# Sample states of a hybrid decoder: from one sequence a step to 128-row chunks of four sequences, with outer products in row groups of the array

## The chip, the cores and the metric

One core of a Trainium2 chip runs the whole program. The metric is the time of one execution in microseconds of the device; three runs of the kernel before the change have a median of 2565.08 us. A difference of some 0.2% (5 us) can be told from none.

## The reference, cut to what matters

One layer of a decoder is computed for a prompt of 512 tokens and for eight sample sequences of four tokens each (32 sample tokens), together 544 columns. Both go through one input projection and then through two branches, an mLSTM and a sliding-window attention, which are merged. The part that changes here is the mLSTM of the sample sequences: each of 8 sequences and 4 heads has a state matrix C of 512 x 512 numbers in f32 (1 MB), which is read, used and written back:

```
num   = s @ v + inter * (q @ C)          # q: 4 tokens of the sequence
den   = sum(s) + inter * (q @ n)
h     = num / max(|den|, exp(-m_row))
C_new = decay * C + (w * k).T @ v        # a sum of four outer products
n_new = decay * n + sum(w * k)
```

So for each head and sequence there is a readout q @ C, and an update of C by a product whose contraction runs over the four tokens of that sequence alone.

## The kernel before

Weights are streamed from memory in pieces of 1024 x 128. A piece is split by ScalarE and VectorE into a high and a low part (`wh`, `wl`, type fp32r), and a product of f32 precision is made of three fp32r products (wh with both parts of the input, wl with the high part). The input projection runs in pairs of column blocks by Strassen's scheme with seven products: `paired` goes through 72 pairs, each of seven half products, and a half product is 24 matmuls of 128 x 128 by 272 columns (L597 with wh, L599 with wl). Two buffers each for wh and wl let the splits run up to two half products ahead.

All other work is written as generators. After each half product `tick()` advances every live generator by one `yield`, so a `yield` is worth one half product of TensorE's time. TensorE keeps the order in which the program is written (`manual_schedule`); the orders of VectorE, ScalarE, GpSimd and the DMA queue are made by a scheduler that simulates the program, and each engine then runs its list strictly in order.

The sample stage (`samples`, `sample_head`) runs beside the later pairs (its TensorE work stands from half product 282 to 487 of 504), head after head:

- `sample_prep` loads q, k, v and n of the 32 sample tokens, repeats k four times over the 128 rows (`rep`, by GpSimd, one quarter for each of four parts), makes scores against q (L969), transposes (L974), and builds `kA`, `Pst` and `V4`: rows of weighted k, of scores and of v in which the four groups of 32 rows hold hi or lo parts, so that one contraction over 128 rows sums the products hi*hi, hi*lo, lo*hi and lo*lo of all 32 tokens.
- Then eight steps, one for each sequence b. GpSimd makes `qz` (q with all but the sequence's columns zero, L1064 and L1065) and `Ab` (`kA` masked to the sequence, L1067). Four half products later TensorE makes the readout (L1079): four f32 products, one for each 128 rows of C, in the four column groups of the array, and they add up in one bank `pC` over all eight steps. Behind it come four outer products (L1085), two at once and two one half product later, each of 128 rows by 128 columns by 512; VectorE adds each to the state (L1086).
- `sample_finish` scales the readout (L1028), sums the four groups by a product with a selection matrix (L1035), adds `num`, normalises by rows (`layernorm_rows`, the tiles `lns`, `lnst`; its last step on ScalarE is L930), and transposes (L1043) three half products later.

States are loaded one step ahead (`load_C`, 1 MB, two buffers) and stored as two DMAs of 512 KB. `sm()` gives one of four banks of PSUM in turn. When all heads are done, the stage's memory is given back and eleven tiles `pf` of the next stage's input are fetched ahead.

Of the kernel before, what the change touches and what calls it, by code (L numbers as in the profile page):

```python
# [21 lines left out]
SEQ = 512  # L22
# [17 lines left out]
SLOPES = [float(np.float32(2.0 ** (-8.0 * (h + 1) / AH))) for h in range(AH)]  # L40


C_ID, C_TRI, C_DIST, C_SB, C_M8, C_SM, C_SEL, C_Q, C_N = 0, 128, 256, 512, 644, 652, 684, 716, 844


def constants():
    c = np.zeros((128, C_N), np.float32)
    p = np.arange(128)
    c[:, C_ID:C_ID + 128] = np.eye(128)
    c[:, C_TRI:C_TRI + 128] = np.where(p[None, :] >= p[:, None], 0.0, NEG)  # L50
    dist = p[:, None] + 128 - np.arange(256)[None, :]
    c[:, C_DIST:C_DIST + 256] = np.where((dist >= 0) & (dist < 128), dist, 1.0e32)
    t = p % 4
    sd = 128 + t[:, None] - np.arange(132)[None, :]
    slope = np.array(SLOPES, np.float32)[p // 4]
# [5 lines left out]
    same = (tok[:, None] // 4 == tt[None, :] // 4) & (tok[:, None] <= tt[None, :])  # L61
    c[:, C_SM:C_SM + 32] = np.where(same, 0.0, NEG)
    c[:, C_SEL:C_SEL + 32] = (tok[:, None] == tt[None, :])
    c[:, C_Q:C_Q + 128] = np.where(tok[:, None] == tok[None, :], 0.25, 0.0)
    return c

# [7 lines left out]
def _build(tc, nc, i, o, es):  # L74
# [83 lines left out]
    dcb = cst.tile([128, MH, NB], F32, name="dcb")  # L158
    dcc = cst.tile([8, MH], F32, name="dcc")
    m8r = cst.tile([128, 8], F32R, name="m8r")  # L160

    d_brm = dr.tile([16, 128, T], F32, name="d_brm")
    d_bra = dr.tile([16, 128, T], F32, name="d_bra")
# [149 lines left out]
    V.memset(r32(m8r[:]), 0.0)  # L313
    for q in (0, 2):
        A.copy(m8r[q * 32:q * 32 + 32], cc[q * 32:q * 32 + 32, C_M8:C_M8 + 8])


    def gates_half(ps, half):
# [19 lines left out]
    def gates(ps):  # L338
# [85 lines left out]
        V.tensor_copy(T1[96:100, 0:128], A3)  # L424

        reps = []
        for src in (T2, T1):
            rep = ev(128)
            V.tensor_copy(rep[:].rearrange("p (r t) -> p r t", r=4),
                          src[:, SEQ:T].unsqueeze(1).to_broadcast([128, 4, NS]))  # L430
            reps.append(rep)
        for _ in range(4):
            yield
        for src, rep, dst, m in ((T2, reps[0], colT2, 3), (T1, reps[1], colT1, 4)):
            pt, pt2 = sm(), sm()
            for b in range(4):
                PE.transpose(pt[:, b * 128:b * 128 + 128], src[:, b * 128:b * 128 + 128], ident)
            PE.transpose(pt2[:, 0:128], rep[:], ident)
            V.tensor_copy(dst[:, 0:4], pt[:].rearrange("p (b d x) -> p b d x", b=4, d=4)[:, :, 0:m, 0:4])
            V.tensor_copy(dst[:, 4], pt2[:, 0:128].rearrange("p (d x) -> p d x", d=4)[:, 0:m, 0:4])  # L440
        pd = sm()
# [502 lines left out]
    def w512():  # L944
        return sp["sw"].tile([128, 512], F32, tag="w", name=nm("w"))

    def load_C(h, b):
        ct = sp["sC"].tile([128, 4, 512], F32, tag="C", name=nm("C"))
        nc.sync.dma_start(ct[:], i["state_mlstm_C"][b, h].rearrange("(c p) v -> p c v", p=128))
        return ct  # L950

    def sample_prep(h, r):
        qs = st1([128, 4, NS], "qs", p="sw")
# [6 lines left out]
        nc.sync.dma_start(nh, i["state_mlstm_n"][:, h, :])  # L960
        yield
        yield
        rep = st1([128, 4, 4, NS], "rep")
        G.tensor_copy(rep[:], ks_[:].unsqueeze(2).to_broadcast([128, 4, 4, NS]))
        yield

        pS, pb = sm(), sm()
        for c in range(4):
            PE.matmul(pS[:, 0:NS], rep[:, c].rearrange("p r t -> p (r t)"), qs[:, c], start=(c == 0), stop=(c == 3))  # L969
        PE.matmul(pb[:, 0:NS], cc[0:4, C_ID + h:C_ID + h + 1].to_broadcast([4, 128]), nM[:, SEQ:T],  # L970
                  start=True, stop=True)
        pk = sm()
        for c in range(4):
            PE.transpose(pk[:, c * 128:c * 128 + 128], rep[:, c].rearrange("p r t -> p (r t)"), ident)  # L974
        ds = st1([128, NS], "ds")
        V.tensor_tensor(out=ds[:], in0=pb[:, 0:NS], in1=cc[:, C_SM:C_SM + NS], op=ALU.add)
        A.activation(ds[:], ds[:], AF.Exp, bias=colT1[:, 4, 0, h:h + 1])
        V.tensor_tensor(out=ds[:], in0=pS[:, 0:NS], in1=ds[:], op=ALU.mult)
        Pst = st1([128, NS], "Pst", F32R)
        A.copy(Pst[:], ds[:])  # L980
        V.tensor_tensor(out=Pst[64:128], in0=ds[64:128], in1=r32(Pst[64:128]), op=ALU.subtract)

        wcol = colT2[:, 4, 2, h:h + 1]
        kA = st1([128, 512], "kA", F32R)
        A.activation(kA[:], pk[:], AF.Copy, scale=wcol)
        V.scalar_tensor_tensor(kA[64:128], pk[64:128], wcol[64:128], r32(kA[64:128]), op0=ALU.mult, op1=ALU.subtract)
        repv = st1([128, 4, 4, NS], "rep")
        G.tensor_copy(repv[:], vs[:].unsqueeze(2).to_broadcast([128, 4, 4, NS]))
        yield

        pvv = sm()
        for c in range(4):
            PE.transpose(pvv[:, c * 128:c * 128 + 128], repv[:, c].rearrange("p r t -> p (r t)"), ident)
        V4 = st1([128, 512], "V4", F32R)
        A.copy(V4[:], pvv[:])
        for q in (1, 3):
            rr = slice(q * 32, q * 32 + 32)
            V.tensor_tensor(out=V4[rr], in0=pvv[rr], in1=r32(V4[rr]), op=ALU.subtract)

        pn = sm()  # L1000
        for c in range(4):
# [18 lines left out]
        pN = sm()  # L1020
        PE.matmul(pN[:NS, :], Pst[:], V4[:], start=True, stop=True)
        num = st1([128, 4, 4, NS], "rep")[:32].rearrange("p c r t -> p (c r t)")
        A.copy(num, pN[:NS, :])
        r.update(kA=kA, V4=V4, den=den, num=num, qs=qs)

    def sample_finish(h, r, pC):
        qc = w512()
        A.activation(qc[:], pC[:], AF.Copy, scale=colT2[:, 4, 1, h:h + 1])  # L1028
# [4 lines left out]
        num, den = r["num"], r["den"]  # L1033
        pI = sm()
        PE.matmul(pI[:NS, :], cc[:, C_SEL:C_SEL + 32], qc[:], start=True, stop=True)  # L1035
        V.tensor_tensor(out=num, in0=pI[:NS, :], in1=num, op=ALU.add)
        hn = w512()[:32]
        layernorm_rows(NS, den[:, 9:10], colT2[0:32, 4, 0, h:h + 1], [num], hn, sp["sw"])
        for _ in range(3):
            yield  # L1040
        pt = sm()
        for c in range(4):
# [3 lines left out]

    def sample_head(h):
        r = {}
        nxt = load_C(h, 0)
        yield from sample_prep(h, r)  # L1050
        pC, stores = None, []
# [8 lines left out]
        for b in range(NB):  # L1060
            ct = nxt

            qz = st1([128, 4, NS], "qz", p="sw")
            G.memset(qz[:], 0.0)  # L1064
            G.tensor_copy(qz[:, :, b * 4:b * 4 + 4], r["qs"][:, :, b * 4:b * 4 + 4])  # L1065
            Ab = st1([128, 512], "Ab", F32R)
            G.tensor_scalar(Ab[:], r32(r["kA"][:]), cc[:, C_M8 + b:C_M8 + b + 1], None, op0=ALU.mult)  # L1067
            for j in range(4):
                yield
                if j == 0:  # L1070
                    store()
                elif j == 2 and b + 1 < NB:
                    with tc.issue_after(state["load"].ins):
                        nxt = load_C(h, b + 1)
            if b == 0:
                pC = sm()

            for c in range(4):
                PE.matmul(pC[c * 32:c * 32 + 32, :], qz[:, c], ct[:, c],  # L1079
                          start=(b == 0), stop=(b == NB - 1), tile_position=(0, c * 32))  # L1080
            for c in range(4):
                if c == 2:
                    yield
                pu = sm()
                PE.matmul(pu[:], Ab[:, c * 128:c * 128 + 128], r["V4"][:], start=True, stop=True)  # L1085
                V.scalar_tensor_tensor(ct[:, c], ct[:, c], dcb[:, h, b:b + 1], pu[:], op0=ALU.mult, op1=ALU.add)  # L1086
                if c % 2:
                    stores.append((C_s[b, h, (c - 1) * 128:c * 128 + 128, :].rearrange("(c p) v -> p c v", p=128),
                                   ct[:, c - 1:c + 1]))
        yield  # L1090
        store()
        while h not in gated:
            yield
        yield from sample_finish(h, r, pC)

    chain_, gated = [], []
    esF, ahead, PF = ExitStack(), [], 11
# [505 lines left out]
```

## Time and profile before

| What | Value |
|---|---|
| Runs | 2562.29, 2565.08, 2566.04 us |
| Profiled execution | span 2561.7 us; no other time is given for it |
| Paired stage | 88.7 us to 1825.4 us (L597 first start, end of the last L599's eight) |
| Sample stage, first load of C to the last transposes | 1047.2 us to 1774.0 us |
| Readouts L1079 | 256 records (each f32 product counts twice), 592/605/617 ns (min/median/max) |
| Outer products L1085 | 128 records, 387/396/498 ns |
| State additions L1086 (VectorE) | 128, 742 ns median |

A row of the timeline holds the start, how long the merged group lasted, the engine, the line, and out<-in with the tiles' shapes; `128*32` is the size of the stationary operand (rows*columns). Since matmuls overlap, the spacing of starts says what each costs. PEld is the load of weights. A row ends with the engine's idle time before it and what released it. A row of a table by windows holds the busy time of each engine with its number of instructions, then the granted clock of TensorE, the busy share of the DMA engines and GB/s.

### The profile page before, as it was taken

How to read it: one execution, taken by the hardware profiler on the slowest of the kernel's cores; microseconds unless marked ns; L12 is line 12 of the kernel's file. 1: busy time of each engine (PE TensorE's matmuls, PEld its weight loads, DVE VectorE, ACT ScalarE, POOL GpSimd, SP SyncE). 2: the span in 40 equal slices, each digit the busy share in tenths (PEclk: the TensorE clock that was granted, in tenths of full speed). 3: DMA queues.
4: the chain of work that ended last, by engine and by line, in shares of the span. 5: the costliest groups of instructions: out<-in, count | busy, mean ns of one | idle time of the engine just before them, and what ended most of it. 6: DMA issues, size and time to landing. Idle time of an engine off the chain costs nothing.

```text
span 2561.7 us, 48818 instructions
## 1 busy us (share of the span) xinstructions
PE 2524.2 (99%) x19994; PEld 2464.3 (96%) x19994; DVE 1707.2 (67%) x2508; ACT 1173.2 (46%) x1908; POOL 362.3 (14%) x334
## 2 busy tenths in 40 slices
PE   8999999999999999999999999999999999999997
PEld 8999999999999999899999998999999999999997
DVE  7867777777777777687777877777856553333236
ACT  4447667666666655333433433434633332222221
POOL 2111211211111111121121222221000000000002
PEclk9999999999999999999999999999999999999999
DMA  6566666666666663477576575676655455446332
GB/s 196 139 160 157 151 156 154 152 158 148 157 160 146 156 161 89 119 230 235 154 236 212 168 227 163 185 235 207 187 171 172 162 179 155 139 135 189 106 97 86
DMA packets 537103, 421.86 MB, mean 165 GB/s; under 512 B 43536, under 2 KB 449344, under 8 KB 536592
## 3 DMA queue, kind: packets, MB, share of 16 engines
q1 hardware_dynamic: 526800, 382.04, 49.8%
q0 software_dynamic: 10080, 36.70, 7.9%
q8 instruction: 157, 2.57, 0.4%
q14 instruction: 66, 0.54, 0.1%
HBM read 297.66 MB, written 86.42 MB: 150 GB/s over the span
## 4 chain that ended last, share of the span: by engine, by line
PE 57%; DVE 1%; issue 0%; POOL 0%; ACT 0%; DVEq 0%
PE mm L200 21%; PE bank L597 17%; PE bank L599 9%; PE sm L1266 2%; PE sm L1085 1%; PE sm L1079 1%; PE sm L1298 1%; PE sm L1311 1%; PE sm L200 1%; DVE z L1505 0%; PE sm L1245 0%; PE sm L1321 0%; PE sm L1253 0%; DVE z L1510 0%; PE sm L1448 0%
## 5 line engine op out<-in xcount | busy, mean ns | idle before, releaser
L191 ACT CAST wh<-raw 128x1024 fp32r<-128x1024 f32 x604 | 632.8, 1048 | 978.5 <-PE bank L597 599.3
L192 DVE TENSOR_TENSOR wl<-raw,wh 128x1024 fp32r<-128x1024 f32 x604 | 750.1, 1243 | 367.3 <-ACT wh L191 359.9
L597 PE MATMUL bank<-xk,wh 128*128 128x272 f32 x2304 | 312.7, 288 | 1.3 <-DVE ev L622 1.3
L597 PEld LDWEIGHTS bank<-xk,wh 128*128 128x128 f32 x2304 | 297.7, 188 | 4.2 <-ACT wh L191 2.4
L577 DVE TENSOR_TENSOR raw<-raw,raw 128x1024 f32<-128x1024 f32 x218 | 276.5, 1270 | 5.5 <-DMA raw<-in_w_in 2.9
L200 PE MATMUL mm<-bh,wl 128*128 128x272 f32 x1024 | 214.0, 289 | 0.0
L200 PE MATMUL mm<-bh,wh 128*128 128x272 f32 x1024 | 213.6, 290 | 0.0
L200 PE MATMUL mm<-bl,wh 128*128 128x272 f32 x1024 | 213.3, 288 | 0.0
L599 PE MATMUL bank<-xk,wl 128*128 128x272 f32 x1152 | 168.1, 288 | 0.0
L616 POOL TENSOR_TENSOR ev<-p,ev 128x272 f32<-128x272 f32 x72 | 105.0, 1458 | 424.9 <-ACT ev L615 404.4
L200 PEld LDWEIGHTS mm<-bh,wh 128*128 128x128 f32 x1024 | 160.7, 188 | 2.3 <-issue 2.3
L200 PEld LDWEIGHTS mm<-bl,wh 128*128 128x128 f32 x1024 | 161.4, 188 | 0.0
L200 PEld LDWEIGHTS mm<-bh,wl 128*128 128x128 f32 x1024 | 160.9, 189 | 0.0
L599 PEld LDWEIGHTS bank<-xk,wl 128*128 128x128 f32 x1152 | 153.4, 189 | 0.0
L597 PE MATMUL bank<-n2h,wh 128*128 128x272 f32 x576 | 149.1, 290 | 1.9 <-ACT wh L191 1.9
L597 PE MATMUL bank<-s1h,wh 128*128 128x272 f32 x576 | 150.5, 292 | 0.0
L597 PE MATMUL bank<-s1l,wh 128*128 128x272 f32 x576 | 149.3, 292 | 0.0
L597 PE MATMUL bank<-s4h,wh 128*128 128x272 f32 x576 | 149.0, 290 | 0.0
L597 PE MATMUL bank<-a11h,wh 128*128 128x272 f32 x576 | 148.7, 290 | 0.0
L597 PE MATMUL bank<-n2l,wh 128*128 128x272 f32 x576 | 148.7, 291 | 0.0
L597 PE MATMUL bank<-a11l,wh 128*128 128x272 f32 x576 | 148.5, 291 | 0.0
L597 PE MATMUL bank<-n3l,wh 128*128 128x272 f32 x576 | 148.2, 290 | 0.0
(427 smaller groups left out, 5489.7 us busy)
## 6 DMA issues: line engine op xcount, KB each, us to landing
raw<-in_w_in SPq DMA_DIRECT2D x296, 512.0 KB, 4.4
raw<-raw POOLq DMA_DIRECT2D x70, 512.0 KB, 4.9
C<-in_state_mlstm_C SPq DMA_DIRECT2D x32, 1024.0 KB, 5.6
out<-C SPq DMA_DIRECT2D x64, 512.0 KB, 3.8
raw<-in_w_proj_a SPq DMA_DIRECT2D x32, 512.0 KB, 5.6
raw<-in_w_proj_m SPq DMA_DIRECT2D x32, 512.0 KB, 4.3
raw<-in_w_out SPq DMA_DIRECT2D x32, 512.0 KB, 4.3
d_sgm<-ev SPq DMA_DIRECT2D x16, 272.0 KB, 3.9
```

Source lines behind the costliest of these rows:

```text
L191: A.copy(wh[:], raw[:])
L192: V.tensor_tensor(out=wl[:], in0=raw[:], in1=r32(wh[:]), op=ALU.subtract)
L200: PE.matmul(ps[:, f, :w], a[:, kk], b(k, c, w), start=(k == 0 and n == 0), stop=(k == 15 and n == 2))
L577: V.tensor_tensor(out=w[out][:], in0=w[a][:], in1=w[b][:], op=ALU.add)
L597: PE.matmul(ps, wh[:, k], x(p, k), start=(first and k == 0 and p == 0), stop=False, skip_group_check=True)
L599: PE.matmul(ps, wl[:, k], x(0, k), start=False, stop=(k == 7), skip_group_check=True)
L616: G.tensor_tensor(out=c22, in0=p1, in1=c11, op=ALU.subtract)
L1079: PE.matmul(pC[c * 32:c * 32 + 32, :], qz[:, c], ct[:, c], start=(b == 0), stop=(b == NB - 1), tile_position=(0, c * 32))
L1085: PE.matmul(pu[:], Ab[:, c * 128:c * 128 + 128], r["V4"][:], start=True, stop=True)
L1266: PE.matmul(pp[:, 0:258], a[:, b * 128:b * 128 + 128], b_[:, b, f], start=(b == 0 and n == 0), stop=(b == 3 and n == 2))
L1298: PE.matmul(pp[:, 0:n], x_[c][:, b * 128:b * 128 + 128], y_[c][:, b * 128:SEQ], start=(c == 0 and m == 0), stop=(c == 3 and m == 2))
L1311: PE.matmul(pp[:, 0:258], x_[:, off:off + 128], y_[:, b, f], start=(b == 0 and n == 0), stop=(b == j and n == 2))
```

## The change

A step no longer takes one sequence with all 512 rows of its C, but 128 rows (chunk c) of four sequences: the even ones for s = 0, then the odd ones for s = 1. `load_C` fetches four blocks of 128 x 512, again 1 MB, and the stores are again two of 512 KB.

```
-    def load_C(h, b):
+    def load_C(h, s, c):
         ct = sp["sC"].tile([128, 4, 512], F32, tag="C", name=nm("C"))
-        nc.sync.dma_start(ct[:], i["state_mlstm_C"][b, h].rearrange("(c p) v -> p c v", p=128))
+        nc.sync.dma_start(ct[:], i["state_mlstm_C"][s::2, h, c * 128:c * 128 + 128, :].rearrange("b p v -> p b v"))
```

The rows of `kA`, `V4` and `Pst` are ordered anew: row group b holds 16 rows (four tokens by four parts) of sequence 2b and 16 of 2b + 1, and `Ab` masks one of the two by s, so it is made twice a head and not eight times. Building the rows takes two ScalarE passes and one VectorE pass:

```
+    def rows_of_parts(out, hi, ps, at, scales):
+        low = st1([128, 512], "rep")
+        A.activation(hi[:], ps[:], AF.Copy, scale=scales[0])
+        A.activation(low[:], ps[:], AF.Copy, scale=scales[1])
+        V.scalar_tensor_tensor(out[:], r32(hi[:]), cc[:, at:at + 1], low[:], op0=ALU.mult, op1=ALU.add)
```

The step itself: the readout of a chunk goes to a bank of its own, is copied out by ScalarE and added up by GpSimd in `sum`; one half product later the four outer products follow together, each with a contraction over the 32 rows of one row group and into a bank of its own.

```
-            for c in range(4):
-                PE.matmul(pC[c * 32:c * 32 + 32, :], qz[:, c], ct[:, c],
-                          start=(b == 0), stop=(b == NB - 1), tile_position=(0, c * 32))
-            for c in range(4):
-                if c == 2:
-                    yield
-                pu = sm()
-                PE.matmul(pu[:], Ab[:, c * 128:c * 128 + 128], r["V4"][:], start=True, stop=True)
-                V.scalar_tensor_tensor(ct[:, c], ct[:, c], dcb[:, h, b:b + 1], pu[:], op0=ALU.mult, op1=ALU.add)
+                pC = sm()
+                for b in range(4):
+                    PE.matmul(pC[b * 32:b * 32 + 32, :], qz[:, b], ct[:, b], start=True, stop=True,
+                              tile_position=(0, b * 32))
+                if (s, c) == (0, 0):
+                    r["sum"] = st1([128, 512], "rep")
+                    A.copy(r["sum"][:], pC[:])
+                else:
+                    some = w512()
+                    A.copy(some[:], pC[:])
+                    G.tensor_tensor(out=r["sum"][:], in0=r["sum"][:], in1=some[:], op=ALU.add)
+                yield
+                pus = [sm() for _ in range(4)]
+                for b in range(4):
+                    rows = slice(b * 32, b * 32 + 32)
+                    PE.matmul(pus[b][:], Ab[rows, c * 128:c * 128 + 128], r["V4"][rows], start=True, stop=True,
+                              tile_position=(b * 32, 0))
+                for b in range(4):
+                    V.scalar_tensor_tensor(ct[:, b], ct[:, b], dcb[:, h, b * 2 + s:b * 2 + s + 1], pus[b][:],
+                                           op0=ALU.mult, op1=ALU.add)
```

`qz` takes four small copies and not one. In `sample_prep` one `yield` is added behind each of the two copies of `rep`, and the one ahead of the product Pst * V4 falls away: that product moves into `sample_finish`, where it adds to the selection product in the same bank, so `num` is gone. In `sample_finish` five half products and not three lie between the normalisation and the transposes. A head thus takes 55 half products and not 52, counted from head to head. In the constants the mask of scores and some columns are laid out anew, and the gates make one more transposed copy of a column (`colW`).

**The order on TensorE at one step.** Before, in the third step of the first head: the end of a half product, the readout (L1079), two outer products (L1085), the next half product.

```order
L599 MATMUL bank_13251<-n3h_122,wl_13247 128x272 x8
L1079 MATMUL sm_12968<-C_13118,qz_13205 32x512 x4
L1085 MATMUL sm_13349<-V_1690_12734,Ab_13208 128x512
L1085 MATMUL sm_13352<-V_1690_12734,Ab_13208 128x512
L597 MATMUL bank_13215<-s4h_1010,wh_13277 128x272
L597 MATMUL bank_13215<-s4l_1011,wh_13277 128x272
```

With the change, in the third step of the first head (L610 and L612 are the old L597 and L599, L1101 is the readout), the readout stands alone:

```order
L612 MATMUL bank_13216<-s4h_1009,wl_13297 128x272 x8
L1101 MATMUL sm_13393<-C_13169,qz_13257 32x512 x4
L610 MATMUL bank_13268<-xk_5_112,wh_13329 128x272
L610 MATMUL bank_13268<-xk_7_114,wh_13329 128x272
L610 MATMUL bank_13268<-xk_5_112,wh_13329 128x272
```

One half product later all four outer products (L1114) stand together:

```order
L612 MATMUL bank_13268<-xk_5_112,wl_13330 128x272 x4
L612 MATMUL bank_13268<-xk_6_113,wl_13330 128x272 x4
L1114 MATMUL sm_13438<-V_1703_12810,Ab_12866 128x512
L1114 MATMUL sm_13439<-V_1703_12810,Ab_12866 128x512
L1114 MATMUL sm_13440<-V_1703_12810,Ab_12866 128x512
L1114 MATMUL sm_13441<-V_1703_12810,Ab_12866 128x512
L610 MATMUL bank_13461<-a11h_108,wh_13364 128x272
L610 MATMUL bank_13461<-a11l_109,wh_13364 128x272
```

Two visits a step remain, but the second pair has moved from one to the other.

**The order at the end of the third head.** Before, on VectorE, the last two steps of the normalisation (L925, L926) stand behind the split wl_18472:

```order
L922 SCALAR_TENSOR_TENSOR lns_18391<-lns_18391 32x1
L192 TENSOR_TENSOR wl_18436<-raw_2477_18433,wh_18435 128x1024
L923 TENSOR_SCALAR lns_18391<-lns_18391 32x1
L192 TENSOR_TENSOR wl_18472<-raw_18325,wh_18471 128x1024
L925 TENSOR_TENSOR lns_18391<-lns_18391 32x1
L926 SCALAR_TENSOR_TENSOR lns_18391<-lns_18391 32x1
```

and on TensorE the transposes (L1043) stand behind the half product that reads wl_18405, from whose buffer wl_18472 has to be made, two splits later:

```order
L597 MATMUL bank_18475<-a11l_108,wh_18404 128x272
L599 MATMUL bank_18475<-a11h_107,wl_18405 128x272 x8
L1043 MATMUL sm_18502<-cc,w_18390 128x32 x4
L597 MATMUL bank_18524<-s1h_118,wh_18435 128x272
L597 MATMUL bank_18524<-s1l_119,wh_18435 128x272
```

With the change the same steps (L938, L939) stand behind the split wl_18843:

```order
L199 TENSOR_TENSOR wl_18807<-raw_2543_18804,wh_18806 128x1024
L938 TENSOR_TENSOR lns_18762<-lns_18762 32x1
L199 TENSOR_TENSOR wl_18843<-raw_18696,wh_18842 128x1024
L939 SCALAR_TENSOR_TENSOR lns_18762<-lns_18762 32x1
L199 TENSOR_TENSOR wl_18874<-raw_2536_18731,wh_18873 128x1024
```

and the transposes (L1064) stand behind the half product that reads wl_18843 itself:

```order
L610 MATMUL bank_18912<-n2l_122,wh_18842 128x272
L612 MATMUL bank_18912<-n2h_121,wl_18843 128x272 x8
L1064 MATMUL sm_18938<-cc,w_18761 128x32 x4
L610 MATMUL bank_18846<-xk_5_112,wh_18873 128x272
L610 MATMUL bank_18846<-xk_7_114,wh_18873 128x272
```

The chain's end has moved ahead of the transposes by two half products, as counted in splits of wl.

**The order on VectorE at one step.** Before, the four additions to the state (L1086) stand in two pairs with other work between:

```order
L192 TENSOR_TENSOR wl_13313<-raw_1742_13062,wh_13312 128x1024
L1086 SCALAR_TENSOR_TENSOR C_13118<-C_13118,dcb,sm_13349 128x512
L1086 SCALAR_TENSOR_TENSOR C_13118<-C_13118,dcb,sm_13352 128x512
L577 TENSOR_TENSOR raw_1785_13395<-raw_13281,raw_13283 128x1024
L577 TENSOR_TENSOR raw_13283<-raw_13283,raw_1775_13316 128x1024
L624 SCALAR_TENSOR_TENSOR ev_13241<-bank_13215,ev_13241 128x272
L192 TENSOR_TENSOR wl_13356<-raw_13281,wh_13355 128x1024
L1086 SCALAR_TENSOR_TENSOR C_13118<-C_13118,dcb,sm_13384 128x512
L1086 SCALAR_TENSOR_TENSOR C_13118<-C_13118,dcb,sm_13387 128x512
```

With the change (L1117) they stand in one piece, behind the split for the half product two ahead:

```order
L199 TENSOR_TENSOR wl_13404<-raw_1787_13401,wh_13403 128x1024
L1117 SCALAR_TENSOR_TENSOR C_13169<-C_13169,dcb,sm_13438 128x512
L1117 SCALAR_TENSOR_TENSOR C_13169<-C_13169,dcb,sm_13439 128x512
L1117 SCALAR_TENSOR_TENSOR C_13169<-C_13169,dcb,sm_13440 128x512
L1117 SCALAR_TENSOR_TENSOR C_13169<-C_13169,dcb,sm_13441 128x512
L199 TENSOR_TENSOR wl_13458<-raw_13300,wh_13457 128x1024
```

All four have moved behind one split, and nothing stands between them.

More of the change, by code (lines that the diff above doesn't have):

```diff
@@ L1018, in sample_prep, with sample_finish @@
         nc.sync.dma_start(n_s[:, h, :], nh)
-        yield
[L1020 to L1026, printed above, removed]
+        r.update(kA=kA, V4=V4, Pst=Pst, den=den, qs=qs)
+    def sample_finish(h, r):
         qc = w512()
-        A.activation(qc[:], pC[:], AF.Copy, scale=colT2[:, 4, 1, h:h + 1])
+        A.activation(qc[:], r["sum"][:], AF.Copy, scale=colT2[:, 4, 1, h:h + 1])
         gs = st1([128, 4, NS], "gs", p="sw")
@@ L1032, in sample_finish @@
         yield
[L1033 removed]
         pI = sm()
[L1035 to L1036 removed]
+        PE.matmul(pI[:NS, :], cc[:, C_SEL:C_SEL + 32], qc[:], start=True, stop=False)
+        PE.matmul(pI[:NS, :], r["Pst"][:], r["V4"][:], start=False, stop=True)
         hn = w512()[:32]
[L1038 to L1039 removed]
+        layernorm_rows(NS, r["den"][:, 9:10], colT2[0:32, 4, 0, h:h + 1], [pI[:NS, :]], hn, sp["sw"])
+        for _ in range(5):
             yield
```

118 lines of the change are left out of this document (67 added, 51 removed).

## Prediction

> **What bounds the kernel now.** I read the page's busy shares first, then its chain of work that ended last, then a table of busy time for a stretch inside the sample stage, and then the timeline of TensorE, instruction by instruction.
>
> ```profile
> span 2561.7 us, 48818 instructions
> PE 2524.2 (99%) x19994; PEld 2464.3 (96%) x19994; DVE 1707.2 (67%) x2508; ACT 1173.2 (46%) x1908; POOL 362.3 (14%) x334
> PE 57%; DVE 1%; issue 0%; POOL 0%; ACT 0%; DVEq 0%
> ...
> core 0: us, PE busy (x) PEld busy (x) DVE busy (x) ACT busy (x) POOL busy (x), PEclk, DMA share, GB/s
> 1200.00:1400.00 200.00, 198.82 (x1533) 185.74 (x1531) 153.10 (x183) 75.31 (x93) 36.43 (x38) 1.00 0.66 207
> ```
>
> TensorE is busy from end to end, and in the sample stage nearly all the time, while VectorE has 47 us of 200 free, ScalarE 125 and GpSimd 164. So a microsecond of TensorE's own sequence is a microsecond of the kernel, as long as nobody makes TensorE wait. Busy time hides two things, though: pipelined products overlap, so their spacing counts and not their length; and TensorE works at half clock after a long wait. Both need the timeline.
>
> ```profile
> 1080.65 1.16 PE L599 MATMUL bank<-a11h,wl 128*128 128x272 f32 x8
> 1081.65 0.29 PE L597 MATMUL bank<-s1h,wh 128*128 128x272 f32 x1
> ...
> 1083.66 1.16 PE L599 MATMUL bank<-s1h,wl 128*128 128x272 f32 x8
> 1084.75 1.06 PE L1079 MATMUL sm<-C,qz 128*32 128x512 f32 x8
> 1085.74 0.72 PE L1085 MATMUL sm<-V,Ab 128*128 128x512 f32 x2
> 1086.31 0.29 PE L597 MATMUL bank<-n2h,wh 128*128 128x272 f32 x1
> ...
> 1088.32 1.16 PE L599 MATMUL bank<-n2h,wl 128*128 128x272 f32 x8
> 1089.32 0.63 PE L1085 MATMUL sm<-V,Ab 128*128 128x512 f32 x2
> 1089.79 2.17 PE L597 MATMUL bank<-xk,wh 128*128 128x272 f32 x16
> 1091.80 0.42 PE L599 MATMUL bank<-xk,wl 128*128 128x272 f32 x2
> ```
>
> The first column is the start. Eight pair products take 1.00 us (1080.65 to 1081.65), sixteen 2.01 (1089.79 to 1091.80), so 0.125 us each and 3.0 us for a half product of 24. One step of a sample head is what stands between them: 0.09 us to enter (1.09 instead of 1.00 before 1084.75), 0.99 for the readouts, 0.57 for two outer products, and in the next visit 0.47 for the other two: 2.12 us, and 32 steps make 68 us.
>
> **The outer products.** Today four products of 512 columns run one after the other; 0.47 us for a pair gives 0.235 us each. The first of a step costs 0.10 more, since it follows the readouts. Without that, which the readouts cause, four cost 0.94 us. After the change each has a contraction of 32 rows and its own row group and bank. Do groups run side by side? The trace has that for columns, and once for rows of 64 together with columns of 32:
>
> ```profile
> L1079 PE MATMUL sm<-C,qz x256: 592/605/617, 1084.7 to 1749.9; 128*32 128x512 f32 x128
> ...
> L1085 PE MATMUL sm<-V,Ab x128: 387/396/498, 1085.7 to 1754.2; 128*128 128x512 f32 x128
> ...
> 954.03 0.44 PE L856 MATMUL sm<-kT,qas 64*32 64x128 f32 x8
> ```
>
> Eight readout products of 605 ns stand within 1.06 us (the f32 product counts twice), so four run at a time; at 954.03 eight products of 64 rows lie within 0.44. I take it that four row groups overlap in the same way. Then an outer visit is one product, 0.235 us, plus about 0.03 for three staggered starts, plus X, the price of changing to row groups and back. No row shows X for fp32r products. Two rows bound it:
>
> ```profile
> 1072.40 0.39 PE L1021 MATMUL sm<-V,Pst 128*32 128x512 f32 x1
> 1072.63 0.28 PE L597 MATMUL bank<-s4h,wh 128*128 128x272 f32 x1
> ...
> 1217.99 1.16 PE L599 MATMUL bank<-s4h,wl 128*128 128x272 f32 x8
> 1219.08 1.04 PE L1035 MATMUL sm<-w,cc 128*32 128x512 f32 x2
> 1220.06 2.28 PE L597 MATMUL bank<-xk,wh 128*128 128x272 f32 x16
> 1222.18 1.17 PE L599 MATMUL bank<-xk,wl 128*128 128x272 f32 x8
> ```
>
> L1021, a narrow fp32r product without a position in the array, costs 0.23 us in all: X is zero. L1035, f32, is entered 0.09 late, lasts 0.98 where the readouts' first pass (half of it) implies about 0.89, and the sixteen products behind it take 2.12 instead of 2.01: 0.29 us for a round trip. I take X = 0.25, near the second, because it also changes what the array is set to. An outer visit then costs 0.235 + 0.03 + 0.25 = 0.52 us, 0.42 less than 0.94, and 32 of them save **13.3 us** (with X from 0 to 0.29: 21.6 to 12.3). The readouts keep their eight products and their round trip of 0.29, now paid towards pair products instead of the first outer product: no change.
>
> [...]
>
> **The waits.** The added half products stand between dependent pieces of a head's start and end. Here the trace has three waits:
>
> ```profile
> 1052.38 1.18 PE L599 MATMUL bank<-s1h,wl 128*128 128x272 f32 x8
> 1057.38 1.92 PE L969 MATMUL sm<-qs,rep 128*128 128x32 f32 x8 [3.82 <-POOL rep L964]
> ...
> 1228.21 1.16 PE L599 MATMUL bank<-s1h,wl 128*128 128x272 f32 x8
> 1230.55 0.43 PE L1043 MATMUL sm<-cc,w 32*128 32x32 f32 x4 [1.18 <-ACT w L930]
> ...
> 1587.09 1.16 PE L599 MATMUL bank<-a11h,wl 128*128 128x272 f32 x8
> 1592.13 0.63 PE L1043 MATMUL sm<-cc,w 32*128 32x32 f32 x4 [3.89 <-ACT w L930]
> ...
> 1057.40:1062.80 5.40, 5.40 (x24) 5.27 (x25) 1.24 (x4) 1.11 (x3) 0.90 (x2) 0.50 0.47 115
> ...
> 1592.10:1598.70 6.60, 6.57 (x30) 6.51 (x31) 0.39 (x2) 1.20 (x2) 0.61 (x1) 0.50 0.23 60
> ...
> 1588.41 2.03 DVE L192 TENSOR_TENSOR wl<-raw,wh 128x1024 fp32r<-128x1024 f32 x1 [0.18 <-ACT wh L191]
> 1590.90 0.15 DVE L925 TENSOR_TENSOR lns<-lns 32x1 f32<-32x1 f32 x1 [0.46 <-POOL lns L924]
> ```
>
> Starting from the end of the eight (start plus 1.00), TensorE lost 4.0, 1.3 and 4.0 us. Behind the two long ones the granted clock is 0.50 for 5.4 and 6.6 us. There 24 and 30 products stand, 0.22 us apart instead of 0.125, so 43% of each stretch is lost: 2.3 and 2.8. Together **14.4 us**.
>
> The last two belong to the end of a head: VectorE's normalisation chain (L925, L926) stands behind the split wl of the second next half product, and that split needs a buffer that TensorE frees only when it reaches the transposes L1043. TensorE waits for a chain that had waited for TensorE. In the changed order two more half products lie between. For the third head the chain stands behind wl_18843, which the half product just ahead of the transposes reads itself; its buffer is free two half products, 6 us, earlier, and the 4.0 us go with 2 to spare. The other heads read alike, so 1.3, 4.0 and 2.8 go. At the first head's start one half product (3.0 us) is added ahead of L969, but GpSimd makes four more small copies ahead of rep there:
>
> ```profile
> 1056.71 0.61 POOL L964 COPY rep<-ks 128x512 f32<-128x512 f32 x1
> ...
> L1065 POOL COPY qz<-qs 128x16 f32<-128x16 f32 x32 | 11.7, 368 | 1.9
> L1067 POOL TENSOR_SCALAR Ab<-kA,cc 128x512 fp32r<-128x512 f32 x32 | 66.4, 2074 | 104.3 <-PE sm L1085 73.6 <-DVE raw L577 20.5 <-DVE ev L622 3.7
> L1028 ACT ACTIVATE w<-sm,colT 128x512 f32<-128x512 f32 x4 | 2.8, 690 | 2.5 <-PE sm L1079 2.5
> L1086 DVE SCALAR_TENSOR_TENSOR C<-C,dcb,sm 128x512 f32<-128x512 f32 x128 | 89.6, 741 | 1.4
> L192 DVE TENSOR_TENSOR wl<-raw,wh 128x1024 fp32r<-128x1024 f32 x207 | 257.8, 1247 | 91.5 <-ACT wh L191 85.9 <-PE bank L599 5.5
> ```
>
> rep would end near 1057.3 + 1.0 (four copies at about a quarter us) = 1058.3, TensorE would ask at 1056.4: 1.9 us stay, too short to lower the clock (the wait of 1.3 did not: clock 1.00 in the 200 us stretch above). So **12.5 us** of 14.4 go; from 10 (should a fifth of them stay elsewhere) to all.
>
> **What is added.** Per step: one ScalarE copy of a bank, 0.69 us at most (L1028); a GpSimd sum, which I bound by Ab's 2.07, a pass over as many elements, and of which one takes the place of an Ab in three steps of four; three small GpSimd copies. All lie beside 15 us of pair products. The one that matters is the copy: the fourth outer product takes the bank that the readouts just left, and TensorE reaches it one half product, 3.0 us, later. In ScalarE's changed order the copy stands behind a split whose buffer is free before the readouts start, so it ends about 1.9 us after they start: nothing. Without that cover, behind the next split, it would cost about 0.7 a step, 24 us. VectorE's four accumulations now stand together, 4 x 0.74 = 3.0 us, but behind the split two half products ahead; the following split (1.25) is due some 8 us later: nothing. In each head's start the chain from the first transposes to the second copy of rep is longer by a ScalarE pass and has 6 us instead of 3: I put 1 us for all four heads. Loads and stores of the state keep their number and size (32 of 1 MB, 64 of 512 KB) and the 2 KB rows, and the 15 us between steps. The heads end 12 half products later, five ahead of the end of the paired stage instead of 17; the prefetch of the branch input moves with them and is still issued ahead of its first use: nothing. Sum: -13.3 - 12.5 + 1.0 = **-24.8 us**, from 2561.7 to 2536.9. That is the span of the profiled execution, the only time given for it; the median of the runs, 2565.1, lies 3.4 above, so I forecast **2540**. Its own range, from the ends above, is 2529 (X = 0, all waits gone) to 2547.
>
> **Rivals.**
> 1. The waits come back in other places, since every order on VectorE, ScalarE and GpSimd was made anew; only the outer products gain. For it: three such waits exist now. Against: the chains in the new order. 2565.1 - 13.3 + 1 = **2553**.
> 2. The row groups do not overlap, and the change does not do what it says: 4 x 0.235 + 0.25 = 1.19 us a visit, 0.25 more than now, +8 us in 32 steps, against 11.5 net from the waits: -3.5, **2562**. Against it speak the column groups. [...]
> 3. Slower: row groups of fp32r neither overlap nor keep the fp32r pace, but take the two passes of the f32 readouts, 0.99 / 2 or about 0.45 us each pass without the ends. Four outer products then cost 4 x 0.9 + 0.25 = 3.85 us, 2.9 more than now, 93 us in all, less 12: **2646**. It decides from a visit of 1.3 us on, where 32 steps lose the 12 us of the waits. For it: no row shows fp32r in a row group. Against: fp32r keeps its pace in the narrow L1021.
>
> **Chances.** Forecast 0.70; rival 1 0.12, rival 2 0.10, rival 3 0.08. Measurement tells some 0.2% or 5 us from no change. The forecast and rival 1 are faster (0.81, with a little for their edges), rival 2 is within 0.2% (0.11), rival 3 slower (0.08). To leave out no more than two in ten the range takes in rivals 1 and 2: 2529 to 2563.
>
> **What would show it.** On the timeline: the four outer products within some 0.03 us of each other and the next pair product 0.4 to 0.6 us after the first start; steps of 1.6 to 1.8 us instead of 2.12; no wait of TensorE over 2 us in the sample stage, and granted clock 1.00 there. Wrong would be outer products 0.23 us or more apart (rival 2 or 3), a wait before the fourth of them (the copy), or new waits at the transposes or at the end of the paired stage.

## The result, and the profile after

Four runs of each kernel give **2547.39 us** for the changed kernel (2543.75 to 2551.11) against 2565.56 us before (2562.29 to 2568.26): ratio **0.9923**, 95% interval [0.9905, 0.9941]. It is faster by some 18 to 20 us, 0.8%. The forecast was 2540 us, 25 us faster; its sign and its mechanisms came out, but two of its terms were too large.

Of the page of the changed kernel, the span and the busy shares:

```profile
span 2541.9 us, 48994 instructions
PE 2509.8 (99%) x19995; PEld 2443.5 (96%) x19995; DVE 1709.8 (67%) x2506; ACT 1195.5 (47%) x1945; POOL 377.4 (15%) x434
```

Of its table of busy time, the row for the same 200 us of the sample stage as before (columns as there):

```profile
1200.00:1400.00 200.00, 200.00 (x1574) 185.89 (x1573) 155.05 (x184) 82.62 (x105) 42.65 (x68) 1.00 0.69 210
```

The outer products' line by itself (shortest, median and longest in ns, first and last start, shape):

```profile
L1114 PE MATMUL sm<-V,Ab x128: 489/497/500, 1089.6 to 1762.8; 32*128 32x512 f32 x128
```

The number of products is the same but for one (19995). In the 200 us window TensorE has no idle time left (1.18 us before) and gets through 1574 products instead of 1533. The extra ScalarE copies and GpSimd sums show as 7 and 6 us more of busy time in that window, and no TensorE wait names them. One step of a sample head, on the timeline of the changed kernel (start, duration, engine, line, what is computed from what):

```profile
1119.14 1.07 PE L1101 MATMUL sm<-C,qz 128*32 128x512 f32 x8
1120.14 2.29 PE L610 MATMUL bank<-xk,wh 128*128 128x272 f32 x16
1122.27 1.16 PE L612 MATMUL bank<-xk,wl 128*128 128x272 f32 x8
1123.35 0.51 PE L1114 MATMUL sm<-V,Ab 32*128 32x512 f32 x4
1123.79 0.39 PE L610 MATMUL bank<-a11h,wh 128*128 128x272 f32 x1
1124.01 0.29 PE L610 MATMUL bank<-a11l,wh 128*128 128x272 f32 x1
...
1123.35 0.19 PEld L1114 LDWEIGHTS sm<-V,Ab 32*128 32x128 f32 x4
1123.78 0.19 PEld L610 LDWEIGHTS bank<-a11h,wh 128*128 128x128 f32 x1 [0.24 <-issue]
```

Four products of 0.49 to 0.50 us lie within 0.51: the row groups do run side by side. But the edges are dear. The eight products before L1114 take 1.08 us instead of 1.00 (+0.09, unrounded), the first pair product starts 0.44 behind the first outer product where a product's own spacing is 0.23, and the second pair product comes 0.23 after the first, not 0.125. The weight loads go with that: at both edges the load starts together with its product and not during the product ahead of it. Over the 32 steps the outer visit costs a median of 0.635 us and the readout visit 1.20, together 1.84 instead of 2.13. That is 58.6 us against 68.0: **9.4 us** saved.

The waits, by the two kernels' lists of TensorE's waits in the sample stage (for what, us in all, how often, the longest). Before:

```profile
PE sm L1043 <- ACT w L930: 5.1, 2, 3.9
PE sm L969 <- POOL rep L964: 3.8, 1, 3.8
```

After:

```profile
PE sm L1000 <- POOL rep L972: 2.4, 1, 2.4
```

The place itself on the timeline of the changed kernel, TensorE first and then GpSimd:

```profile
1054.24 1.17 PE L612 MATMUL bank<-n2h,wl 128*128 128x272 f32 x8
1057.78 1.39 PE L1000 MATMUL sm<-qs,rep 128*128 128x32 f32 x8 [2.37 <-POOL rep L972]
1068.65 0.60 PE L1023 MATMUL sm<-cc,rep 128*128 128x128 f32 x4
...
1054.33 2.86 POOL L1091 COPY qz<-qs 128x4 f32<-128x4 f32 x6
1057.12 0.61 POOL L972 COPY rep<-ks 128x512 f32<-128x512 f32 x1
```

And the busy time and clock behind it:

```profile
1057.40:1065.20 7.80, 7.42 (x35) 7.29 (x36) 1.55 (x5) 2.40 (x5) 1.19 (x4) 0.56 0.53 136
```

The waits at the end of the heads are gone. The one at the first head's start is shorter, 2.5 us instead of 4.0, but the clock still falls behind it: from L1000 to L1023 the first head takes 10.87 us, the other three 7.73. (A wait is counted here from the spacing of products, as in the prediction; the bracketed idle time starts at the modelled end of the last product and is some 0.17 us less.) So that place still costs 2.5 + 3.1 = 5.7 us, and of the waits' 14.4 us some 9 have gone.

### The profile page after: what moved, and what is told of

It is laid out like the page before. It is cut to its first block, busy times and chain, and to the rows that moved or that the text cites. A ratio compares the mean times of both kernels' runs of the same rounds, so it can differ in the third digit from the quotient of the medians.

```text
span 2541.9 us, 48994 instructions
## 1 busy us (share of the span) xinstructions
PE 2509.8 (99%) x19995; PEld 2443.5 (96%) x19995; DVE 1709.8 (67%) x2506; ACT 1195.5 (47%) x1945; POOL 377.4 (15%) x434
## 4 chain that ended last, share of the span: by engine, by line
PE 57%; DVE 1%; issue 0%; POOL 0%; DVEq 0%
PE mm L207 21%; PE bank L610 18%; PE bank L612 9%; PE sm L1298 2%; PE sm L1101 1%; PE sm L1330 1%; PE sm L1343 1%; PE sm L207 1%; PE sm L1114 1%; DVE z L1537 0%; PE sm L1277 0%; PE sm L1285 0%; PE sm L1353 0%; DVE z L1542 0%; PE sm L1480 0%
## 5 line engine op out<-in xcount | busy, mean ns | idle before, releaser
L610 PE MATMUL bank<-xk,wh 128*128 128x272 f32 x2304 | 318.3, 291 | 0.0
L610 PEld LDWEIGHTS bank<-xk,wh 128*128 128x128 f32 x2304 | 299.5, 189 | 10.0 <-ACT wh L198 7.5
L612 PE MATMUL bank<-xk,wl 128*128 128x272 f32 x1152 | 167.5, 288 | 0.0
L612 PEld LDWEIGHTS bank<-xk,wl 128*128 128x128 f32 x1152 | 154.1, 189 | 0.0
L610 PE MATMUL bank<-n2h,wh 128*128 128x272 f32 x576 | 148.9, 291 | 2.0 <-ACT wh L198 2.0
L610 PE MATMUL bank<-a11h,wh 128*128 128x272 f32 x576 | 149.3, 291 | 0.0
L610 PE MATMUL bank<-s1h,wh 128*128 128x272 f32 x576 | 149.1, 292 | 0.1
L610 PE MATMUL bank<-s4h,wh 128*128 128x272 f32 x576 | 149.0, 292 | 0.0
L610 PE MATMUL bank<-n3h,wh 128*128 128x272 f32 x576 | 148.1, 290 | 0.0
L610 PE MATMUL bank<-a11l,wh 128*128 128x272 f32 x576 | 147.9, 289 | 0.0
L610 PE MATMUL bank<-n2l,wh 128*128 128x272 f32 x576 | 147.3, 288 | 0.0
L610 PE MATMUL bank<-n3l,wh 128*128 128x272 f32 x576 | 146.8, 287 | 0.0
```

The source lines that it names most:

```text
L610: PE.matmul(ps, wh[:, k], x(p, k), start=(first and k == 0 and p == 0), stop=False, skip_group_check=True)
L612: PE.matmul(ps, wl[:, k], x(0, k), start=False, stop=(k == 7), skip_group_check=True)
```

## The experiments

All are compared with runs of the kernel before on the same chip. Experiments 1, 3, 4 and 5 make one group (median of before 2567.6 us), 2, 6 and 7 another (2566.1 us).

**1. The half products alone.** The kernel before, with only its yields set as in the changed kernel (four added, one taken out, 55 half products a head); the sample state, its readouts and its outer products stay as they were.

```diff
         G.tensor_copy(rep[:], ks_[:].unsqueeze(2).to_broadcast([128, 4, 4, NS]))
+        yield
...
         G.tensor_copy(repv[:], vs[:].unsqueeze(2).to_broadcast([128, 4, 4, NS]))
+        yield
...
-        yield
         pN = sm()
...
-        for _ in range(3):
+        for _ in range(5):
```

> The kernel before with nothing but the added half products: one more behind each of the two copies of rep, five and not three ahead of a head's transposes, and the one ahead of Pst * V4 taken out, so that a head takes 55 half products as in the changed kernel. Theory (waits and the half clock behind them are one half of the gain, row groups the other): the two waits at the transposes (1.3 and 4.0 us, with 2.8 us of half clock) go, the wait at the first head's start shrinks to about 1 us and leaves the clock alone, since GpSimd has no four extra copies here: 13 us faster than before, ratio 0.995. Rival (the waits come back in other places, all of the gain is that of the row groups): no change, ratio 1.000.

Measured: 2554.16 us, ratio 0.9940 [0.9928, 0.9953]. The interval holds the theory's 0.995 and leaves out the rival. TensorE's only wait left in the sample stage:

```profile
PE sm L970 <- POOL rep L964: 0.8, 1, 0.8
```

The waits were worth about what the trace before said: 15 us by the ratio, 12 us by the two traces. Against the expectation, the clock did fall behind the wait of 1 us that stayed (0.57 from 1058 to 1062 us, last section), so 2.6 us are still lost at the first head.

**2. The changed kernel without the added half products.**

```diff
         rep = four_parts(ks_)
         yield
-        yield
...
         repv = four_parts(vs)
         yield
-        yield
...
-        for _ in range(5):
+        for _ in range(3):
```

> The changed kernel without its added half products: one between the copy of rep and the scores and one between the copy of repv and the products with it, instead of two and two, and three instead of five ahead of a head's end. Only the outer products have changed against the kernel before. Theory: the outer products alone bring 9.4 us, the waits at the transposes stay small by the new order on VectorE (at most about 1 us each), and the first head's start waits some 3 us longer than in the changed kernel (about 5.5 us, then half clock): ratio to the kernel before about 0.995. Rival 1: every wait of the kernel before is back, the outer products alone count: 0.9965. Rival 2: the outer products bring the 13.3 us forecast and the waits at the transposes are gone: 0.992.

Measured: 2549.54 us, ratio 0.9938 [0.9925, 0.9952]. The interval holds the theory's 0.995 and leaves out both rivals, 0.9965 clearly and 0.992 by little. On its timeline, the chain's end and the transposes of the third head, where the kernel before lost 4.0 us; then the first head's end, and the start of the first head:

```profile
1572.45 0.15 DVE L939 SCALAR_TENSOR_TENSOR lns<-lns 32x1 f32<-32x1 f32 x1
1575.59 1.16 PE L612 MATMUL bank<-n3h,wl 128*128 128x272 f32 x8
1576.68 0.43 PE L1062 MATMUL sm<-cc,w 32*128 32x32 f32 x4
...
1229.43 0.43 PE L1062 MATMUL sm<-cc,w 32*128 32x32 f32 x4 [0.85 <-ACT w L943]
...
1061.07 1.91 PE L999 MATMUL sm<-qs,rep 128*128 128x32 f32 x8 [4.29 <-POOL rep L972]
```

VectorE's chain ends 4.1 us ahead of the transposes, without any added half product. So the waits at the head's end go with either part of the change: the reordered heads already take the chain out from behind the late split, and the added half products would have done it alone (experiment 1). Which of the reordered pieces does it was not tested. That is why the two parts, 15 and 16 us each by itself, make 20 and not 31 together.

**3. The row groups alone.** The changed kernel, with its outer products over all 128 rows and no position in the array. Every state then takes in the products of all four sequences of its chunk.

```diff
-                    rows = slice(b * 32, b * 32 + 32)
-                    PE.matmul(pus[b][:], Ab[rows, c * 128:c * 128 + 128], r["V4"][rows], start=True, stop=True,
-                              tile_position=(b * 32, 0))
+                    PE.matmul(pus[b][:], Ab[:, c * 128:c * 128 + 128], r["V4"][:], start=True, stop=True)
```

> The changed kernel with the four outer products of a step as four products over all 128 rows, one after the other, without a position in the array; each then sums the four sequences of the chunk, so the updated states are not the reference's. Theory (row groups overlap, and the visit costs 0.39 us on top of one product): a visit grows from 0.63 to 0.94 us, 32 of them 10 us: ratio to before about 0.996. Rival of my forecast (a visit with row groups should cost 0.52): 13 us, ratio 0.9975. Rival (row groups bring nothing, all of the gain is in the waits): as the changed kernel, 0.992.

Measured: 2555.26 us, ratio 0.9951 [0.9939, 0.9964], with the theory's 0.996 inside and both rivals outside, so the row groups are worth about 0.3%. The timeline of this kernel, at such a visit:

```profile
1124.99 1.16 PE L612 MATMUL bank<-xk,wl 128*128 128x272 f32 x8
1125.98 1.09 PE L1113 MATMUL sm<-V,Ab 128*128 128x512 f32 x4
1126.91 0.29 PE L610 MATMUL bank<-a11h,wh 128*128 128x272 f32 x1
...
1125.86 0.77 PEld L1113 LDWEIGHTS sm<-V,Ab 128*128 128x128 f32 x4
1126.68 0.19 PEld L610 LDWEIGHTS bank<-a11h,wh 128*128 128x128 f32 x1
```

Without a position there is no edge: 0.99 for the eight products ahead, 0.93 for four outer products, and both weight loads start 0.12 and 0.23 us ahead of their products. 0.93 against 0.635 is what the row groups save per step, 9.3 us in 32.

**4. Two visits of two groups each.** The changed kernel, with a half product between the second and the third outer product, and one half product fewer ahead of the readouts.

```diff
-                for j in range(4):
+                for j in range(3):
...
-                pus = [sm() for _ in range(4)]
+                pus = []
                 for b in range(4):
+                    if b == 2:
+                        yield
+                    pus.append(sm())
...
-                for b in range(4):
```

> The changed kernel with the four row groups in two visits of two, one half product apart; a half product less ahead of the readout, so that a step stays at five. Theory (a visit costs one product and 0.39 us to change to row groups and back, however many groups it holds): 0.63 us more a step, 20 us in 32 steps, ratio to before about 1.000. With 0.25 us for the change, as forecast: 0.49 us a step, 16 us, 0.9985. If the 0.39 us belong to four banks written at once and not to the change: two groups cost half of it, 0.24 us more a step, 8 us, 0.9955.

Measured: 2565.89 us, ratio 0.9994 [0.9984, 1.0004]. On the timeline both visits of a step:

```profile
1128.86 1.16 PE L612 MATMUL bank<-s4h,wl 128*128 128x272 f32 x8
1129.94 0.50 PE L1117 MATMUL sm<-V,Ab 32*128 32x512 f32 x2
1132.49 1.16 PE L612 MATMUL bank<-xk,wl 128*128 128x272 f32 x8
1133.59 0.50 PE L1117 MATMUL sm<-V,Ab 32*128 32x512 f32 x2
```

The interval still holds the forecast's 0.9985, so the visits have to decide: a visit of two costs a median of 0.627 us, a visit of four 0.635, and with X = 0.25 one of two would cost 0.49. The price belongs to the visit and not to the number of groups: one visit more per step eats the whole gain of the change.

**5. One more half product ahead of the first head's scores.**

```diff
         yield
+        if h == 0:
+            yield
```

> The changed kernel with one more half product between the first head's rep and its scores. Theory (the wait of 2.5 us that stayed there, and the half clock for 6.8 us behind it, worth about 2.9 us): both go, 5.4 us faster than the changed kernel, ratio to before 0.990, granted clock 1.00 through the sample stage. Rival (the clock would fall there anyway, or the wait moves on with the half product): as the changed kernel, 0.992.

Measured: 2538.69 us, ratio 0.9885 [0.9871, 0.9898], somewhat more than the theory's 0.990. On its timeline:

```profile
1061.36 1.16 PE L612 MATMUL bank<-xk,wl 128*128 128x272 f32 x8
1062.36 0.97 PE L1002 MATMUL sm<-qs,rep 128*128 128x32 f32 x8
1070.10 0.60 PE L1025 MATMUL sm<-cc,rep 128*128 128x128 f32 x4
```

In its table of busy time and clock:

```profile
1060.00:1066.00 6.00, 6.00 (x51) 5.92 (x50) 2.86 (x4) 3.14 (x5) 2.10 (x5) 1.00 1.05 248
```

The wait is gone, and so is the stretch at half clock: L1002 to L1025 takes 7.74 us, as in every other head. The half clock goes with the wait: experiment 7, the other kernel without the wait, has none there either (1.00 from 1055 to 1066 us), and behind the wait the granted clock is 0.50 in the kernel before (1056.0 to 1062.8 us), 0.50 in the changed kernel (1058.4 to 1065.2) and 0.57 in experiment 1 (1058 to 1062). By the traces both were worth 5.7 us; the ratios differ by more (9.7 us), within their intervals.

**6. Readouts and outer products in one visit.** The readouts get a PSUM bank of their own, so that the outer products need not wait for the copy, and no half product stands between; it stands ahead of the readouts instead, and a step stays at five. The bank is one of the four that the pair products use (`bank`); the heads keep the four of `sm()`, so rival 2 of the expectation names the wrong ones.

```diff
-        psA["mm"] = pool(esP, "psP" if pairs else "psA", 4 if pairs else 2, PSUM)
+        psA["mm"] = pool(esP, "psP" if pairs else "psA", 3 if pairs else 2, PSUM)
+        if pairs:
+            psA["px"] = pool(esP, "psX", 1, PSUM)
...
-                for j in range(4):
+                for j in range(5):
...
-                pC = sm()
+                pC = psA["px"].tile([128, 512], F32, tag="px", name=nm("px"))
...
-                yield
                 pus = [sm() for _ in range(4)]
```

> The changed kernel with a PSUM bank of its own for the fourth outer product, so that readouts and outer products stand in one visit, without a half product between them. Theory: the cost of a visit lies at its edges; one exit to pair products (about 0.10 for the late weights of the first pair product and 0.09 of draining) and one entry (0.09) less make 0.2 to 0.29 us a step, 6 to 9 us in 32 steps against the changed kernel: ratio to the kernel before 0.989 to 0.990; the four outer products start some 0.1 to 0.2 us behind the last readout's end. Rival: going from f32 column groups to fp32r row groups costs as much as going through pair products: 0.992, as the changed kernel. Rival 2: one PSUM bank fewer for the heads makes TensorE wait at the readouts: above 0.994.

Measured: 2538.32 us, ratio 0.9897 [0.9882, 0.9913]. Its timeline at a visit:

```profile
1122.01 1.06 PE L1103 MATMUL px<-C,qz 128*32 128x512 f32 x8
1123.01 0.50 PE L1115 MATMUL sm<-V,Ab 32*128 32x512 f32 x4
1123.44 0.40 PE L612 MATMUL bank<-a11h,wh 128*128 128x272 f32 x1
1123.67 0.29 PE L612 MATMUL bank<-a11l,wh 128*128 128x272 f32 x1
```

The outer products follow the readouts as closely as pair products do (1.00 us behind their start in both kernels), so going from column groups straight to row groups costs nothing extra. One visit takes 1.636 us (median of 32) where the two took 1.20 + 0.635: 0.20 saved a step, 6.4 us in all, against the 6.7 us that the ratios give. The timelines show how long the edges are; that 0.09 us of them is draining, as the theory has it, no run shows. The missing bank shows no price: from 1000 to 1800 us TensorE's only wait is that of the changed kernel at the first head's start (2.4 us).

**7. Both.** Experiments 5 and 6 together.

> Both the visit in one piece and one more half product ahead of the first head's scores. Theory: the two gains add: 6 to 9 us for the one visit and 6 to 9 us for the first head's wait and half clock against the changed kernel, ratio to the kernel before about 0.985 (0.983 to 0.988). Rival: only the first head's wait counts: 0.9885.

Measured: **2531.79 us**, ratio 0.9867 [0.9853, 0.9881], the fastest of all, 34 us ahead of the kernel before and 14 ahead of the change. The two gains add, within the intervals: 0.9885 and 0.9897, each counted from 0.9923, would give 0.9859. For the same 600 us of the sample stage, the changed kernel:

```profile
1100.00:1700.00 600.00, 600.00 (x4717) 557.68 (x4717) 480.45 (x561) 265.69 (x339) 151.29 (x211) 1.00 0.67 203
```

and this one:

```profile
1100.00:1700.00 600.00, 600.00 (x4760) 561.64 (x4759) 483.68 (x565) 268.98 (x342) 137.53 (x211) 1.00 0.68 207
```

Both have TensorE busy throughout at full clock; only the number of products in it differs (4717 and 4760), as the edges take less time.

## Why the prediction was right, and where its sizes were off

The account of all runs, from their traces: us in the 32 steps, at the first head's start (wait, and the time lost to the clock behind it), and at the heads' ends (with 2.8 us of clock before); their sum against the kernel before; and the measured difference (the ratio's, of 2566 us, with its interval).

| kernel | steps | first start | ends | sum against before | measured |
|---|---|---|---|---|---|
| before | 68.0 | 4.0 + 2.6 | 8.1 | | |
| changed | 58.6 | 2.5 + 3.1 | 0 | -18.5 | -19.8 [-24.4, -15.1] |
| 1 half products alone | 68.0 | 1.0 + 1.7 | 0 | -12.0 | -15.4 [-18.5, -12.1] |
| 2 without them | 58.6 | 4.5 + 3.8 | 1.9 | -13.9 | -15.9 [-19.2, -12.3] |
| 3 whole array | 67.9 | 2.5 + 3.1 | 0 | -9.2 | -12.6 [-15.7, -9.2] |
| 4 two visits | 78.5 | 2.5 + 3.1 | 0 | +1.4 | -1.5 [-4.1, +1.0] |
| 5 first wait | 58.6 | 0 | 0 | -24.1 | -29.5 [-33.1, -26.2] |
| 6 one visit | 52.3 | 2.5 + 3.2 | 0 | -24.7 | -26.4 [-30.3, -22.3] |
| 7 both | 52.3 | 0 | 0 | -30.4 | -34.1 [-37.7, -30.5] |

Every measured difference is 1 to 5 us larger than its sum. Most of that is half clock outside the account. Each timed run lists its mean granted clock, and span times (1 - clock) is what it lost: 21 us on average for the kernel before, whose one trace, on which the sums rest, lost 19; 14, 18, 17, 18, 13, 17 and 10 us for experiments 1 to 7. With the lost clock taken out on both sides, the mean differences are -7.1, -12.5, -7.9, +1.9, -20.3, -22.4 and -22.2, and the sums -8.3, -12.3, -6.9, +3.7, -18.7, -22.5 and -25.0: within 3 us, and no longer all to one side.

- **What bounds the kernel** held: a microsecond of TensorE's own sequence is a microsecond of the time. Experiments 3, 4 and 6 change little else, and come out at their visits' sums.
- **The row groups overlap**, and keep the fp32r pace, as forecast (0.51 us for four); rivals 2 and 3 fall. Rival 1 falls too: no new wait shows in the sample stage, and its 2553 us lies above the interval.
- **The outer products: the mechanism was right, the size off.** The term was -13.3 us and measured -9.4. The step that failed is "I take X = 0.25": a visit takes 0.635 us, of which 0.23 are a product and 0.01 the three starts, so X is 0.39 (0.09 to enter, 0.20 until the first pair product, 0.10 at the second). The upper bound, 0.29, came from f32 column groups, and the trace before had no row for this change. The entry is the 0.09 that L1079 and L1035 had shown before; the price lies on the way out, 0.30 of the 0.39.
- **The waits: 9 us of the 12.5 forecast.** Those at the heads' ends went, to the last, as forecast. Two steps failed at the first head's start. "Four copies at about a quarter us": no row had that price, and the copies of `qz` ahead of rep take 2.86 us for six where the two before took 1.32, so 1.5 us more and not 1.0; 2.5 us of wait stayed instead of 1.9. (The price is not fixed: the same six took 1.79 us in experiment 2.) And "too short to lower the clock": it lowered it (0.50 from 1058.4 to 1065.2 us), for another 3.1 us. The comparison drawn there, with a wait of 1.3 us that had left the clock alone (1.00 from 1228 to 1240 us), did not carry over: waits of 0.82 and 0.85 us had clocks of 0.57 and 1.00 behind them (last section). Experiment 5 shows both amounts together. Half clock at this place cost 2.6 us before, by the other heads' 4.74 us from L969 to the next transposes, where the prediction read 2.3.
- **The reason given for the waits at the ends was one of two.** The added half products were named as what removes them. Experiment 2 shows that the reordered heads leave at most 1.9 us of waits (here and at the copy of repv) without them. In the changed kernel the half products add only about 4 us (0.9923 against 0.9938; the intervals overlap, the traces give 4.6), mostly at the first head.
- **The added work cost nothing**, as forecast: no wait of TensorE names the copy, the sum or VectorE's four additions. The 1 us put down for the longer chain at a head's start did not show either: L1000 to L1023 takes the same 7.73 us in three heads, without a wait.
- **Sum.** -24.8 forecast; -9.4 and -9.1 by the trace, -18.5, where the spans differ by 19.8. The forecast time was 7 us too low, of which 4 lie in X and 3 to 4 in the first head's start. The stated range up to 2563 takes in rivals 1 and 2; of the forecast's own range, 2529 to 2547, the measured time is just past the end. Of the signs named, the steps came out at 1.84 us instead of 1.6 to 1.8, and a wait of over 2 us with half clock behind it stayed.

## What to carry to other kernels

The small products in row groups of the array were paid for by the visit here, not by the product: 0.635 us for a visit of four and 0.627 for one of two (experiment 4), 0.39 of it for the change to row groups and back. So put all grouped products of a step in one visit (0.20 us a step gained here by leaving out the pair work between two kinds of groups), and count visits ahead of products when such a packing is weighed. And a wait at the start of a stage is to be counted with the half clock that may follow: 2.5 us cost 5.7 here, and one more piece of independent work ahead of it brought all of that back (experiment 5).

## What the runs showed of the hardware

**Two waits of nearly one length had different clocks behind them.** In experiment 1 the first head's start, on the timeline:

```profile
1056.49 1.08 PE L970 MATMUL sm<-qs,rep 128*128 128x32 f32 x8 [0.82 <-POOL rep L964]
```

The row of busy time and clock behind it:

```profile
1058.00:1062.00 4.00, 4.00 (x22) 4.00 (x22) 1.19 (x4) 1.12 (x3) 2.19 (x2) 0.57 0.94 232
```

In experiment 2 the stretch around the wait of 0.85 us at 1229.43, shown above:

```profile
1228.00:1240.00 12.00, 11.15 (x91) 10.85 (x89) 6.68 (x7) 5.51 (x8) 1.51 (x1) 1.00 0.45 111
```

Nearly the same wait, 0.82 and 0.85 us, with granted clocks of 0.57 and 1.00 behind them. In the kernel before, the wait of 1.18 us at 1230.55 has 1.00 from 1228 to 1240 us, and those of 3.82 and 3.89 us have 0.50 behind them (1056.0 to 1062.8 and 1591.9 to 1598.6); the changed kernel's 2.37 us has 0.50 from 1058.4 to 1065.2. The timelines of the two short waits differ in the work around them: in experiment 1, narrow products follow the wait (L970 and the two lines after it, 14 products), and 2.75 us lie between the end of the eight pair products ahead and the next pair product; in experiment 2 it is the four of L1062, and 1.38 us. No run varied the narrow products alone, so they go with the clock here, and are not shown to be its cause.

**The clock also falls without a wait.** Just ahead of the sample stage, in code that no experiment touches, stretches at half clock come and go from trace to trace. The same 6 us in the table of busy time of the kernel before:

```profile
1023.00:1029.00 6.00, 6.00 (x51) 5.85 (x50) 2.21 (x5) 1.53 (x3) 0.00 (x0) 1.00 0.32 87
```

And of experiment 4:

```profile
1023.00:1029.00 6.00, 6.00 (x30) 5.62 (x30) 0.72 (x3) 0.53 (x2) 0.00 (x0) 0.50 0.32 87
```

TensorE is busy in both, with 51 products against 30, at granted clocks of 1.00 and 0.50. The same narrow products start at 1020.02 us in one and 1020.05 in the other. What sets the two traces apart was not shown. Such stretches are part of why single profiled spans of these kernels are not comparable to within 5 us (the timed runs of experiment 4 alone lie between 2561.0 and 2571.7), and why the comparisons above rest on timed rounds and on the visits.
